# Conformer-and-attention block on one core: the layer norm of the convolution branch finished inside the attention projection, rarer convolution taps, four buffers for the rotated halves, weights recorded with priority

## The chip, the cores and the metric

The kernel runs on one NeuronCore of a Trainium2 chip. The metric is device time in microseconds (us), the median of three runs. The core has a matrix engine (PE, with its weight loads shown as PEld), a vector engine (DVE), a scalar engine (ACT), a third elementwise engine (POOL) and an engine that here only issues transfers (SP). Each engine works through its own list of instructions in order and waits on semaphores for the others.

## The reference

One decoder block on x of 2048 tokens by 1024 channels, all in fp32:

```python
h = rmsnorm(x, norm_g)
glu_in, conv_gate, q, k, v, attn_gate, merge_logits = split(h @ w_in)   # w_in 1024 x 7680
c = silu(layernorm(causal_depthwise_conv31(a * sigmoid(b))))            # a, b = halves of glu_in
y_conv = (c * silu(conv_gate)) @ w_conv_out
att = sliding_window_attention(rope(q), rope(k), v, sinks)              # 16 heads of 64, 4 kv heads, window 128
y_attn = (att * silu(attn_gate)) @ w_attn_out
g_conv, g_attn = split(sigmoid(merge_logits))
out = rmsnorm(x + (g_conv * y_conv + g_attn * y_attn) @ w_out, final_norm_g)
```

## The kernel before

**Sweeps and tiles.** The tokens go in two sweeps of T = 1024, each in two halves of TH = 512. Channels stand on the 128 partitions, so a projection makes one tile of 128 output channels by 512 tokens from KC = 8 tiles of the contraction. fp32 accuracy is kept by splitting each operand into a high and a low part: `project` issues, for each of the eight k, the three matmuls whi x hT_hi, whi x hT_lo, wlo x hT_hi, so 24 matmuls for one half. Names tell the part: `gb`, `ga` the two halves of glu_in, `ka`/`kb`, `v`, `q_a`/`q_b`, then `ag` (attention gate), `cg` (convolution gate), `ma` and `mc` (the two merge gates), `ya` and `yc` (the projections after attention and convolution), `o` (the last one).

**Weights.** `load_w` (lines 244 to 266) fetches a weight tile in two parts: a DMA into `raw` (L250), a cast on ACT into `whi` (L253), and in sweep 0 a subtraction on POOL into `wlo` (L242), which is stored to DRAM (`d_lo`, L263) and fetched from there in sweep 1. The three staging tags have four buffers each. `prefetch` in `project` calls it one projection ahead. A name such as `whi_ma_21` is merge-gate tile 2, second part.

**Order.** PE's order is written by hand: a `Line` (from L80) adds up a modelled time and, between matmuls, calls background operations (`bg`) at a spacing `every` and late chains (attention blocks, layer norm, the gated products `u`) when they fall due. `CONV_EVERY` is that spacing while the 31 convolution taps per channel tile run (L393, DVE), `LN_EVERY` that of the layer norm. The order on ACT, DVE, POOL and SP is made by a scheduler that takes ready work by priority; `tc.high_priority(offset=PRIO)` moves what is recorded inside it ahead by 60 places of priority.

**Stages of a sweep.** Load and normalise x, transposed into hT (in sweep 0 `build_h_first`: sqf L350, ssf L351, xf L354, tpf L361, hT L363 and L364); gb/ga, k, v, q projections with rope (`rope_items`: products `ra` L461, `rb` L467, combined on POOL, then split on ACT and DVE); then attention in 32 blocks (scores `sc` L566, exponentials L584, scaling L589, transposes tpp, `pt` L599, masked copy `pc` L605, `ov` L614, result `ss` L617 to L624) interleaved with ag, ga/gb, cg, ma projections and with the convolution taps; then mc, the layer norm, ya, yc and o.

**Layer norm.** When the last tap is done, `ln_chain` sums over channels with four matmuls (`lnmu`), `ln_center` subtracts the mean from the eight `cv` tiles and adds up the squares (L671 ACT, L672 DVE), `ln_chain2` sums again (`lnvar`), then four reciprocals (L676), eight `ln_apply` (L679 DVE, L680 ACT Silu), then `u_chain` makes uT (L711 and a split), which yc multiplies. `ya_item` writes its gated result `mp[e]` into the home `C[e]`, where `cv` tile e lives till then, so before it writes, it calls `line.finish()` if `u` of tile e is not stored yet. The last weights `wo` take the homes C[k] from `mp`.

Of the kernel before, what the change touches and what calls it, by code (L numbers as in the profile page):

```python
# [12 lines left out]
F32 = mybir.dt.float32  # L13
F32R = mybir.dt.float32r
I32 = mybir.dt.int32
AF = mybir.ActivationFunctionType
ALU = mybir.AluOpType
AX = mybir.AxisListType

P = 128  # L20
S = 2048
D = 1024
KC = D // P
T = 1024
NSWEEP = S // T
NB = T // P
TH = 512
# [15 lines left out]
LN_EVERY = 1.6  # L43
GLU_AFTER = (0, 6, 12, 16, 19, 22, 25, 28)
ROPE_EVERY = 3.2
CONV_EVERY = 2.4
ATT_EVERY = 13.8
LAT = (22.0, 16.0)
PRIO = 60
# [4 lines left out]
def hybrid_block(ctx: ExitStack, tc: tile.TileContext, x, par_d, w_in, w_conv, sinks, w_attn, w_out,  # L54
# [22 lines left out]
    C = [f"c{i}" for i in range(8)]  # L77
# [3 lines left out]
    def slot(tag, shape, dt, name):  # L81
        n = int(np.prod(shape[1:]))
        full = HALO + T + 2 if tag in WIDE else 1024
        t = slots.tile([P, full], dt, tag=tag, name=name)
        v = t[:, 0:n]
        if len(shape) == 3:
            v = v.rearrange("p (a b) -> p a b", b=shape[2])
        elif len(shape) == 4:
            v = v.rearrange("p (a b c) -> p a b c", b=shape[2], c=shape[3])
        return v  # L90
# [6 lines left out]
    def next_of(key, tags):  # L97
        rot.setdefault(key, cycle(range(len(tags))))
        return tags[next(rot[key])]
# [46 lines left out]
    def lng(c):  # L146
        return par[:, c, TAPS + 2:TAPS + 3]

    def lnb(c):
        return par[:, c, TAPS + 3:TAPS + 4]  # L150
# [93 lines left out]
    def load_w(src, name):  # L244

        parts = []
        at = lo_at.setdefault((src.tensor.name, src.offset), len(lo_at))
        for kh in range(2):
            raw = stage.tile([P, 4, P], F32, tag="raw", name=f"raw_{name}{kh}")
            nc.sync.dma_start(out=raw, in_=src[:, 4 * kh:4 * kh + 4, :])  # L250
            hi = stage.tile([P, 4, P], F32R, tag="whi", name=f"whi_{name}{kh}")
            lo = stage.tile([P, 4, P], F32R, tag="wlo", name=f"wlo_{name}{kh}")
            act.copy(hi, raw)  # L253
            if (at, kh) in lo_stored:
                nc.sync.dma_start(out=f(lo), in_=d_lo[at, kh])
            else:
                split_lo(lo, raw, hi, pool)
            parts.append((hi, lo))

        def keep(kh):  # L260
            if (at, kh) not in lo_stored:
                lo_stored.add((at, kh))
                nc.sync.dma_start(out=d_lo[at, kh], in_=f(parts[kh][1]))  # L263

        return lambda k: (parts[k // 4][0][:, k % 4, :], parts[k // 4][1][:, k % 4, :]), keep

    def project(src, rhs, name, evac, halves=(0, 1)):

        got = {}

        def prefetch():
            got["w"] = load_w(src, name)

        def blocks():
            for half in halves:
                ps = mm_ps.tile([P, TH], F32, tag="mm", name=f"mm_{name}{half}")
                for k in range(KC):
                    whi, wlo = got["w"][0](k)
                    r = rhs(k, half)
                    for i, (a, b) in enumerate(((whi, r[:, 0, :]), (whi, r[:, 1, :]), (wlo, r[:, 0, :]))):  # L280
                        pe.matmul(out=ps, lhsT=a, rhs=b, start=(k == 0 and i == 0),  # L281
                                  stop=(k == KC - 1 and i == 2))
                    if k == KC - 1:
                        with tc.high_priority(offset=PRIO):
                            evac(half, ps)
                    if half == halves[-1] and k % 4 == 3:
                        got["w"][1](k // 4)
                    yield 3 * MM_US

        def by_halves():  # L290
            return [project(src, rhs, f"{name}{h}", evac, (h,)) for h in range(2)]

        return prefetch, blocks, by_halves
# [78 lines left out]
    def sweep(s):  # L372
# [82 lines left out]
        def rope_items(name, e, store):  # L455
            first = {}

            def ev_a(half, ps):
                t = first[half] = slot(AT[4 + half], [P, 2, TH], F32, f"ra{s}_{name}_{half}")
                dve.tensor_tensor(out=t[:, 0, :], in0=ps, in1=cs[half][:, 0, :], op=ALU.mult)  # L460
                dve.tensor_tensor(out=t[:, 1, :], in0=ps, in1=cs[half][:, 1, :], op=ALU.mult)  # L461

            def ev_b(half, ps):
                a = first[half]
                b = slot(next_of("rb", [AT[6], AT[13]]), [P, 2, TH], F32, f"rb{s}_{name}_{half}")
                dve.tensor_tensor(out=b[:, 1, :], in0=ps, in1=cs[half][:, 1, :], op=ALU.mult)
                dve.tensor_tensor(out=b[:, 0, :], in0=ps, in1=cs[half][:, 0, :], op=ALU.mult)  # L467
                pool.tensor_tensor(out=a[:, 0, :], in0=a[:, 0, :], in1=b[:, 1, :], op=ALU.subtract)
                pool.tensor_tensor(out=a[:, 1, :], in0=a[:, 1, :], in1=b[:, 0, :], op=ALU.add)
                for i in range(2):  # L470
                    hl = slot(next_of("hl", AT[7:11]), [P, 2, TH], F32R, f"hl{s}_{name}_{half}_{i}")
                    put_split(hl, a[:, i, :], dve)
                    store(i, half, f(hl))

            return [project(w_in[e], h_rhs, f"{name}a{s}", ev_a),
                    project(w_in[e + 1], h_rhs, f"{name}b{s}", ev_b)]
# [184 lines left out]
        def ln_center(c):  # L661
            dve.tensor_tensor(out=cv[c], in0=cv[c], in1=ln["mu"], op=ALU.subtract)
            if c == 0:
                ln["v"] = work.tile([P, T], F32, tag="ln0", name=f"vsum{s}", bufs=1)
            for half in range(2):
                hs = slice(half * TH, (half + 1) * TH)
                if c == 0:
                    act.activation(out=ln["v"][:, hs], in_=cv[c][:, hs], func=AF.Square)
                else:
                    q = t2k(f"sq{s}_{c}_{half}")  # L670
                    act.activation(out=q, in_=cv[c][:, hs], func=AF.Square)  # L671
                    dve.tensor_tensor(out=ln["v"][:, hs], in0=ln["v"][:, hs], in1=q, op=ALU.add)  # L672

        def ln_recip(i):
            r = ln["r"][:, i * (T // 4):(i + 1) * (T // 4)]
# [2 lines left out]
        def ln_apply(c):  # L678
            dve.tensor_tensor(out=cv[c], in0=cv[c], in1=ln["r"], op=ALU.mult)  # L679
            act.activation(out=cv[c], in_=cv[c], func=AF.Silu, scale=lng(c), bias=lnb(c))  # L680

        def ln_chain():
            parts = ln_parts(csum, "csum")
# [10 lines left out]
        def ln_chain2():  # L694
            parts = ln_parts(ln["v"], "vsum")
            yield 0.0, LN_LAT[1]
            st = ln_stats(parts, "lnvar")
            ln["r"] = slot(X[1], [P, T], F32, f"rstd{s}")
            for half in range(2):
                act.activation(out=ln["r"][:, half * TH:(half + 1) * TH], in_=st[half], func=AF.Sqrt, bias=eps)  # L700
            work_ops = [lambda i=i: ln_recip(i) for i in range(4)]
            line.bg.extend(work_ops + [lambda c=c: ln_apply(c) for c in range(KC)])
            line.late.append((line.t, u_chain(), lambda: len(uT) > 0))
            yield 4 * MM_US, 0.0


# [17 lines left out]
        def u_chain():  # L724
            for e in range(KC):
                line.bg.extend([lambda e=e, h=h: u_op(e, h) for h in range(2)])
            return
            yield
# [55 lines left out]
        def ya_item(e, first):  # L784
            def ev(half, ps):
                if half == 0:
                    if ("u", e, 1) not in stored:
                        line.finish()
                    mp[e] = slot(C[e], [P, T], F32, f"mp{s}_{e}")
                g = load_gate("ma", e, half)  # L790
                dve.tensor_tensor(out=mp[e][:, half * TH:(half + 1) * TH], in0=ps, in1=g, op=ALU.mult)

            prefetch, blocks, _ = project(w_attn[e], lambda k, half: aT[half][k],
                                       f"ya{s}_{e}", ev)
            if not first:
                return prefetch, blocks

            def first_blocks():
                start_u()
                if None in aT[0] + aT[1]:  # L800
                    line.finish()
                yield from blocks()

            return prefetch, first_blocks
# [30 lines left out]
        def load_wo(n, k):  # L835
            raw = raw_tile(f"rawo{s}_{n}_{k}")
            nc.sync.dma_start(out=raw, in_=wout[:, k, n * TH:(n + 1) * TH])
            w = slot(C[k], [P, 2, TH], F32R, f"wo{s}_{n}_{k}")
            act.copy(w[:, 0, :], raw)
            split_lo(w[:, 1, :], raw, w[:, 0, :], dve)  # L840
            wo[(n, k)] = w
# [115 lines left out]
```

## Time and profile before

| what | us |
|---|---|
| median of three runs (lowest, highest) | 2090.49 (2089.47, 2090.71) |
| the profiled execution | 2090.34 |
| its span in the trace | 2088.4 |
| PE busy in the span | 2044.0 (98%) |
| DVE, ACT, POOL busy | 1391.3, 1032.4, 483.2 |
| mean granted clock of PE | 0.995 |

The profiled execution stands 0.15 us under the median, and 1.9 us of it lie outside the span. PE is busy for all but 44.4 us of the span, so what a change can save at constant work is in those 44.4 us and in stretches in which the clock of PE is granted at less than full. The line numbers in all rows of before are those of the listing above; in the changed kernel lines behind L272 stand one to three higher.

### The profile page before, as it was taken

To read this page: it belongs to the slowest core of one execution; us is meant where nothing else is said; L and a number is where in the kernel's file an instruction comes from. 1 tells how busy PE (TensorE), PEld (TensorE's weight loads), DVE (VectorE), ACT (ScalarE), POOL (GpSimd) and SP (SyncE) were. 2 spreads that over 40 slices of the span, in tenths; PEclk is the share of its full clock that TensorE was granted. 3 is DMA by queue.
4 is the path that set the end of the run, shared out by engine and by line. 5 is a ranking of instruction groups with operands and counts; after the bars stand their busy time and mean duration, and the time that the engine had idled before them with its cause. 6 is when DMAs were issued, how large, how long until landed. Compare 5 with 4: busy or idle time off the path is not lost.

```text
span 2088.4 us, 27452 instructions
## 1 busy us (share of the span) xinstructions
PE 2044.0 (98%) x9256; PEld 1671.7 (80%) x9256; DVE 1391.3 (67%) x1901; ACT 1032.4 (49%) x2265; POOL 483.2 (23%) x336
## 2 busy tenths in 40 slices
PE   7999999998999999999999999999999999999998
PEld 6787888886777888888888888888888888888887
DVE  4979779998988348123559596698888934341324
ACT  6221377666667646112442214766777774621222
POOL 2445433433334222243001131121111110000200
PEclk9999999999999999999999999999999999999999
DMA  7344555554455775646344456555555578574432
GB/s 250 133 144 157 178 166 157 158 163 146 148 152 182 254 238 184 202 142 221 101 151 132 141 161 204 172 158 175 175 163 164 175 225 259 162 236 146 140 119 81
DMA packets 265820, 355.90 MB, mean 170 GB/s; under 512 B 28112, under 2 KB 126544, under 8 KB 265680
## 3 DMA queue, kind: packets, MB, share of 16 engines
q1 hardware_dynamic: 265680, 354.16, 53.3%
q8 instruction: 73, 1.20, 0.2%
q14 instruction: 67, 0.55, 0.1%
HBM read 234.51 MB, written 119.54 MB: 170 GB/s over the span
## 4 chain that ended last, share of the span: by engine, by line
PE 70%; DVE 4%; issue 2%; ACT 1%; DMA 0%; POOL 0%; SPq 0%; DVEq 0%; POOLq 0%; ACTq 0%
PE o L877 9%; PE mm_mc L281 8%; PE mm_yc L281 8%; PE mm_ya L281 8%; PE mm_ma L281 7%; PE mm_ga L281 5%; PE mm_cg L281 5%; PE mm_ag L281 4%; PE mm_gb L281 4%; DVE cv L393 2%; PE mm_q_a L281 2%; PE mm_q_b L281 2%; PE ov L614 2%; PE sc L566 2%; PE mm_v L281 1%
## 5 line engine op out<-in xcount | busy, mean ns | idle before, releaser
L393 DVE SCALAR_TENSOR_TENSOR cv<-glu,par,cv 128x1024 f32<-128x1024 f32 x480 | 675.9, 1408 | 6.7
L605 POOL TENSOR_SCALAR_AFFINE_SELECT pc<-pt 128x1024 fp32r<-128x1024 f32 x60 | 102.7, 1711 | 452.9 <-DVE pt L242 419.6
L877 PE MATMUL o<-wo,mT 128*128 128x512 f32 x768 | 181.3, 394 | 0.0
L877 PEld LDWEIGHTS o<-wo,mT 128*128 128x128 f32 x768 | 143.1, 188 | 32.1
L281 PE MATMUL mm_cg<-hT,whi_cg 128*128 128x512 f32 x512 | 163.2, 400 | 4.6 <-ACT glu L415 3.0
L281 PE MATMUL mm_ma<-hT,whi_ma 128*128 128x512 f32 x512 | 162.9, 399 | 4.0 <-ACT whi_ma L253 4.0
L281 PE MATMUL mm_ga<-hT,whi_ga 128*128 128x512 f32 x512 | 161.0, 395 | 0.2 <-ACT whi_ga L253 0.2
L281 PE MATMUL mm_ag<-hT,whi_ag 128*128 128x512 f32 x512 | 160.9, 395 | 0.0
L281 PE MATMUL mm_gb<-hT,whi_gb 128*128 128x512 f32 x512 | 160.6, 395 | 0.0
L281 PE MATMUL mm_mc<-hT,whi_mc 128*128 128x512 f32 x512 | 159.6, 393 | 0.0
L281 PE MATMUL mm_yc<-uT,whi_yc 128*128 128x512 f32 x512 | 159.4, 392 | 0.0
L281 PE MATMUL mm_ya<-aT,whi_ya 128*128 128x512 f32 x512 | 158.7, 391 | 0.0
L281 PEld LDWEIGHTS mm_cg<-hT,whi_cg 128*128 128x128 f32 x512 | 95.3, 191 | 25.2 <-ACT glu L415 3.4
L281 PEld LDWEIGHTS mm_ma<-hT,whi_ma 128*128 128x128 f32 x512 | 95.1, 190 | 23.9 <-ACT whi_ma L253 4.4
L281 PEld LDWEIGHTS mm_yc<-uT,whi_yc 128*128 128x128 f32 x512 | 96.2, 188 | 21.9
L281 PEld LDWEIGHTS mm_mc<-hT,whi_mc 128*128 128x128 f32 x512 | 96.0, 188 | 21.8
L281 PEld LDWEIGHTS mm_ya<-aT,whi_ya 128*128 128x128 f32 x512 | 96.1, 188 | 20.9
L281 PEld LDWEIGHTS mm_ga<-hT,whi_ga 128*128 128x128 f32 x512 | 94.5, 188 | 20.8 <-ACT whi_ga L253 1.0
L281 PEld LDWEIGHTS mm_gb<-hT,whi_gb 128*128 128x128 f32 x512 | 94.7, 188 | 20.0
L281 PEld LDWEIGHTS mm_ag<-hT,whi_ag 128*128 128x128 f32 x512 | 94.2, 188 | 19.7 <-ACT whi_ag L253 0.3
L584 ACT ACTIVATE ss<-ss,st 128x128 f32<-128x128 f32 x256 | 99.9, 391 | 19.2 <-DVE st L579 18.6
L815 POOL TENSOR_TENSOR lmc<-lmc,mp 128x512 f32<-128x512 f32 x32 | 41.9, 1309 | 275.5 <-DVE lmc L814 267.1
(363 smaller groups left out, 4356.4 us busy)
## 6 DMA issues: line engine op xcount, KB each, us to landing
qk<-d_q SPq DMA_DIRECT2D x256, 64.0 KB, 2.7
d_a<-ss SPq DMA_DIRECT2D x128, 128.0 KB, 1.9
aT<-d_a SPq DMA_DIRECT2D x32, 512.0 KB, 6.1
qk<-d_k SPq DMA_DIRECT2D x240, 64.0 KB, 2.1
raw_gb<-in_w_in_dram SPq DMA_DIRECT2D x34, 256.0 KB, 4.0
raw_ga<-in_w_in_dram SPq DMA_DIRECT2D x34, 256.0 KB, 3.4
raw_ag<-in_w_in_dram SPq DMA_DIRECT2D x32, 256.0 KB, 3.8
d_ag<-ag SPq DMA_DIRECT2D x32, 256.0 KB, 2.1
```

What stands on the lines that cost most here:

```text
L281: pe.matmul(out=ps, lhsT=a, rhs=b, start=(k == 0 and i == 0), stop=(k == KC - 1 and i == 2))
L393: dve.scalar_tensor_tensor(out=cv[c], in0=glu[c][:, j:j + T], scalar=tap(c, j), in1=cv[c], op0=ALU.mult, op1=ALU.add)
L566: pe.matmul(out=o, lhsT=q[:, h, :], rhs=r, start=(j == 0), stop=(j == 1))
L584: act.activation(out=sb[:, h, :], in_=sb[:, h, :], func=AF.Exp, scale=SCALE, bias=ngm[:, h:h + 1], accum_out=den[:, h:h + 1])
L605: pool.affine_select(out=pc, in_=f(pt), pattern=[[0, 2], [0, GQ], [1, P]], compare_op=ALU.is_ge, fill=0.0, base=0, channel_multiplier=-1)
L614: pe.matmul(out=ov, lhsT=vv, rhs=pp[:, i % 2], start=(i == 0), stop=(i == nm - 1))
L815: pool.tensor_tensor(out=g, in0=g, in1=mp[e][:, half * TH:(half + 1) * TH], op=ALU.add)
L877: pe.matmul(out=ps, lhsT=a[:, c0:c0 + P], rhs=r, start=(k == 0 and i == 0), stop=(k == KC - 1 and i == 2))
```

## The change

Seven edits. The spacing of convolution taps in the line of PE goes from 2.4 to 2.55 us. The prefetch of every projection weight is recorded with priority. `ra` takes its home in turn from four places instead of one per half. Half of the additions of squares (L672, half 1) go from DVE to POOL. `u_chain` waits for all eight `ln_apply`. `mp` gets the homes X[2], X[0], X[1], C[0] to C[4] in place of C[0] to C[7], and the line is finished only for e = 2 when `ln_apply` isn't through, and for e > 2 when `u` of tile e - 3 isn't. `wo` takes C[5], C[6], C[7], C[0] and so on.

```diff
-CONV_EVERY = 2.4
+CONV_EVERY = 2.55
...
         def prefetch():
-            got["w"] = load_w(src, name)
+            with tc.high_priority(offset=PRIO):
+                got["w"] = load_w(src, name)
...
             def ev_a(half, ps):
-                t = first[half] = slot(AT[4 + half], [P, 2, TH], F32, f"ra{s}_{name}_{half}")
+                t = first[half] = slot(next_of("ra", AT[4:6] + C[4:6]), [P, 2, TH], F32, f"ra{s}_{name}_{half}")
...
-                    dve.tensor_tensor(out=ln["v"][:, hs], in0=ln["v"][:, hs], in1=q, op=ALU.add)
+                    (dve, pool)[half].tensor_tensor(out=ln["v"][:, hs], in0=ln["v"][:, hs], in1=q, op=ALU.add)
...
             act.activation(out=cv[c], in_=cv[c], func=AF.Silu, scale=lng(c), bias=lnb(c))
+            if c == KC - 1:
+                stored.add("applied")
...
-            line.late.append((line.t, u_chain(), lambda: len(uT) > 0))
+            line.late.append((line.t, u_chain(), lambda: len(uT) > 0 and "applied" in stored))
...
-                    if ("u", e, 1) not in stored:
+                    if e > 2 and ("u", e - 3, 1) not in stored or e == 2 and "applied" not in stored:
                         line.finish()
-                    mp[e] = slot(C[e], [P, T], F32, f"mp{s}_{e}")
+                    mp[e] = slot(([X[2], X[0], X[1]] + C)[e], [P, T], F32, f"mp{s}_{e}")
...
-            w = slot(C[k], [P, 2, TH], F32R, f"wo{s}_{n}_{k}")
+            w = slot(C[(k + 5) % KC], [P, 2, TH], F32R, f"wo{s}_{n}_{k}")
```

What this makes of the order is shown at four places. The first is SP's list at the very start: `xf` are the eight row blocks of x, `raw_gb_000` and `_001` the first weight tile. Before:

```order
L107 DMA xf_0_80<-in_x_dram 128x1024
L107 DMA xf_1_82<-in_x_dram 128x1024
L107 DMA xf_2_84<-in_x_dram 128x1024
L107 DMA xf_3_86<-in_x_dram 128x1024
L133 DMA sink_bc<-in_attn_sinks_dram 128x16
L136 DMA par<-in_par_dram 128x280
L453 DMA cs_0_133<-in_rope_dram 128x2x512
L453 DMA cs_1_135<-in_rope_dram 128x2x512
L250 DMA raw_gb_000_137<-in_w_in_dram 128x512
L250 DMA raw_gb_001_143<-in_w_in_dram 128x512
```

and now:

```order
L250 DMA raw_gb_000_137<-in_w_in_dram 128x512
L250 DMA raw_gb_001_143<-in_w_in_dram 128x512
L107 DMA xf_0_80<-in_x_dram 128x1024
L107 DMA xf_1_82<-in_x_dram 128x1024
L107 DMA xf_2_84<-in_x_dram 128x1024
L107 DMA xf_3_86<-in_x_dram 128x1024
L133 DMA sink_bc<-in_attn_sinks_dram 128x16
```

The two weight parts have moved ahead of x. The second place is ACT's list some 20 us later, where the last tiles of the first half of hT are evacuated (`hT_0_6`, `hT_0_7`), the squares of the second half's rows are summed (`sqf`) and the next weights are cast. Before:

```order
L363 ACTIVATE hT_0_6_130<-tpf_6_220,par 128x512
L351 ACTIVATE ssf_234<-ssf_234,eps_t 128x1
L350 ACTIVATE sqf_1_240,ssf_234<-xf_1_151 128x1024
L363 ACTIVATE hT_0_7_131<-tpf_7_227,par 128x512
L351 ACTIVATE ssf_234<-ssf_234,eps_t 128x1
L350 ACTIVATE sqf_2_245,ssf_234<-xf_2_153 128x1024
L350 ACTIVATE sqf_3_250,ssf_234<-xf_3_155 128x1024
L351 ACTIVATE ssf_234<-ssf_234,eps_t 128x1 x2
L253 CAST whi_ga_000_257<-raw_ga_000_255 128x512
```

and now:

```order
L364 ACTIVATE hT_0_6_130<-tpf_6_220,par 128x512
L352 ACTIVATE ssf_234<-ssf_234,eps_t 128x1
L351 ACTIVATE sqf_2_245,ssf_234<-xf_2_153 128x1024
L351 ACTIVATE sqf_3_250,ssf_234<-xf_3_155 128x1024
L253 CAST whi_ga_000_257<-raw_ga_000_255 128x512
L253 CAST whi_ga_001_263<-raw_ga_001_261 128x512
L352 ACTIVATE ssf_234<-ssf_234,eps_t 128x1 x2
L253 CAST whi_ka_299<-raw_ka_297 128x512
L364 ACTIVATE hT_0_7_131<-tpf_7_227,par 128x512
L253 CAST whi_ka_305<-raw_ka_303 128x512
```

`hT_0_7` now stands behind two sums of squares, two roots and three weight casts. The third place is ACT's list in the attention of sweep 0, at the second part of merge-gate tile 2. Before:

```order
L584 ACTIVATE ss_3_1_5355,st_3_1_5358<-ss_3_1_5355,st_3_1_5358 128x128 x3
L599 CAST pt_3_0_5437<-tpp_3_0_5431 128x512
L434 ACT_TABLE_LOAD
L434 ACTIVATE ma_1_0_5443<-mm_ma_10_5407 128x512
L589 ACTIVATE ss_3_1_5355<-ss_3_1_5355,st_3_1_5358 128x128 x4
L617 COPY ss_2_7_5081<-ov_2_7_5457 64x256
L253 CAST whi_ma_21_5403<-raw_ma_21_5401 128x512
```

and now:

```order
L585 ACTIVATE ss_3_1_5346,st_3_1_5349<-ss_3_1_5346,st_3_1_5349 128x128
L253 CAST whi_ma_21_5394<-raw_ma_21_5392 128x512
L585 ACTIVATE ss_3_1_5346,st_3_1_5349<-ss_3_1_5346,st_3_1_5349 128x128 x2
L435 ACT_TABLE_LOAD
L435 ACTIVATE ma_1_0_5434<-mm_ma_10_5398 128x512
L600 CAST pt_3_0_5428<-tpp_3_0_5422 128x512
L590 ACTIVATE ss_3_1_5346<-ss_3_1_5346,st_3_1_5349 128x128 x4
L618 COPY ss_2_7_5070<-ov_2_7_5448 64x256
```

The cast has moved ahead of the scaling L589 and stands among the exponentials; in the same way the casts of ag_61, ga_41, cg_71, gb_71, ga_71 and ma_01 have moved ahead by a few places. The fourth place is PE's list in sweep 0, at the two groups of layer-norm matmuls. Before, the second group stood in merge-gate tile `mc` 6:

```order
L281 MATMUL mm_mc_60_6894<-hT_0_1_125,wlo_mc_60_6813 128x512
L658 MATMUL lnvar_0_6901<-vsumh_0_6708,ones 128x512
L658 MATMUL lnvar_0_6901<-vsuml_0_6709,ones 128x512
L658 MATMUL lnvar_1_6904<-vsumh_1_6712,ones 128x512
L658 MATMUL lnvar_1_6904<-vsuml_1_6713,ones 128x512
L281 MATMUL mm_mc_60_6894<-hT_0_2_126,whi_mc_60_6812 128x512 x2
```

and now it stands in the second half of the first tile of `ya`:

```order
L282 MATMUL mm_ya_01_7079<-aT_1_5_6726,wlo_ya_01_6961 128x512
L659 MATMUL lnvar_0_7099<-vsumh_0_6921,ones 128x512
L659 MATMUL lnvar_0_7099<-vsuml_0_6922,ones 128x512
L659 MATMUL lnvar_1_7102<-vsumh_1_6925,ones 128x512
L659 MATMUL lnvar_1_7102<-vsuml_1_6926,ones 128x512
L282 MATMUL mm_ya_01_7079<-aT_1_6_6754,whi_ya_01_6960 128x512 x2
```

The first group (`lnmu`) has moved in the same way from `mc` 2 to behind the first half of `mc` 5, and in sweep 1 both groups move by about as much. PE's list is otherwise the same. DVE's list keeps its order through rope, and in attention single taps move by one or two places. In the layer norm the half-1 additions are gone from DVE, and the first four `mp` products of `ya` now stand among the reciprocals, the `ln_apply` products and `u`.

## Prediction

> **What bounds the kernel now.** I read the page first, then PE's waits, then stretches, then single moments. PE's row of the page:
>
> ```profile
> PE 2044.0 (98%) x9256; PEld 1671.7 (80%) x9256; DVE 1391.3 (67%) x1901; ACT 1032.4 (49%) x2265; POOL 483.2 (23%) x336
> ```
>
> PE is busy for 2044.0 of 2088.4 us, so the change, which takes no matmul away, can give at most the idle 44.4 us and what a lowered clock costs. The longest of PE's waits behind the head, up to 700 us (engine, line, waited for; us in total, times, longest):
>
> ```profile
> PE mm_ma L281 <- ACT whi_ma L253: 4.0, 1, 4.0
> PE mm_q_b L281 <- DVE rb_q__1_1524 L467: 3.4, 1, 3.4
> PE mm_cg L281 <- ACT glu L415: 3.0, 1, 3.0
> PE tpv L499 <- ACT vs L519: 2.1, 1, 2.1
> PE mm_cg L281 <- POOL wlo_cg L242: 2.0, 1, 2.0
> PE mm_ga L281 <- POOL wlo_ga L242: 1.8, 2, 1.2
> ...
> PE mm_gb L281 <- POOL wlo_gb L242: 1.5, 1, 1.5
> ...
> PE mm_ag L281 <- POOL wlo_ag L242: 1.3, 1, 1.3
> PE mm_q_b L281 <- DVE ra_q__0_1408 L461: 1.3, 1, 1.3
> ...
> PE mm_ma L281 <- POOL wlo_ma L242: 0.6, 1, 0.6
> ```
>
> Six of these rows name a weight part (whi or wlo): 4.0 + 2.0 + 1.8 + 1.5 + 1.3 + 0.6 = 11.2 us, all in the attention of sweep 0. The rest are evacuations (glu, vs) and rope. The stretches (start and length, then busy us of PE, PEld, DVE, ACT, POOL, PE's granted clock, DMA share, GB/s):
>
> ```profile
> 140.00:211.00 71.00, 65.78 (x277) 52.67 (x276) 69.87 (x58) 10.38 (x18) 32.39 (x20) 0.98 0.46 145
> 235.00:640.00 405.00, 386.72 (x1793) 314.95 (x1792) 363.74 (x467) 274.97 (x636) 147.48 (x96) 0.98 0.52 158
> 550.00:560.00 10.00, 8.04 (x35) 6.38 (x34) 9.90 (x14) 4.25 (x10) 5.65 (x3) 0.83 0.44 134
> 620.00:630.00 10.00, 6.03 (x29) 4.71 (x27) 9.82 (x13) 9.46 (x22) 0.09 (x1) 0.95 0.60 180
> 630.00:640.00 10.00, 9.87 (x33) 7.39 (x34) 9.90 (x14) 6.17 (x17) 4.64 (x3) 0.71 0.30 91
> 720.00:1000.00 280.00, 280.00 (x1226) 228.67 (x1225) 114.93 (x148) 97.41 (x160) 81.54 (x60) 1.00 0.59 196
> 1073.00:2080.00 1007.00, 1007.00 (x4571) 827.31 (x4570) 643.12 (x893) 491.46 (x1066) 126.64 (x83) 1.00 0.54 169
> ```
>
> The last row says that sweep 1 has no gap on PE: nothing is to be had there. Rope (140 to 211) and attention (235 to 640) are where PE idles, and there DVE is busy for 69.87 of 71 and 363.74 of 405 us.
>
> **The change part by part.**
>
> **The head: a loss.** Rows of the first 30 us:
>
> ```profile
> 4.28 1.06 ACT L350 ACTIVATE sqf<-xf 128x1024 f32<-128x1024 f32 x1 [1.98 <-DMA xf<-in_x_dram]
> 5.69 1.06 ACT L350 ACTIVATE sqf<-xf 128x1024 f32<-128x1024 f32 x1
> 15.55 1.13 ACT L253 CAST whi_gb<-raw_gb 128x512 fp32r<-128x512 f32 x2
> 18.52 0.70 PE L281 MATMUL mm_gb<-hT,whi_gb 128*128 128x512 f32 x2
> 20.57 0.69 ACT L363 ACTIVATE hT<-tpf,par 128x512 fp32r<-128x512 f32 x1
> 21.30 0.75 DVE L364 SCALAR_TENSOR_TENSOR hT<-tpf,par,hT 128x512 fp32r<-128x512 f32 x1 [0.19 <-ACT hT L363]
> 23.78 0.62 ACT L253 CAST whi_ga<-raw_ga 128x512 fp32r<-128x512 f32 x1
> 24.45 0.73 PE L281 MATMUL mm_ga<-hT,whi_ga 128*128 128x512 f32 x2 [0.21 <-ACT whi_ga L253]
> 25.87 0.50 PE L281 MATMUL mm_ga<-hT,wlo_ga 128*128 128x512 f32 x1 [0.70 <-POOL wlo_ga L242]
> ```
>
> and of DVE's waits behind the head, up to 700 us, the one for PE:
>
> ```profile
> DVE glu L419 <- PE mm_ga L281: 23.9, 5, 9.3
> ```
>
> The first weight tile (two parts of 128x512, as many bytes as one row block of x) now loads ahead of x. Two row blocks start on ACT 5.69 - 4.28 = 1.4 us apart, so x comes about 1.4 us later; the two whi_gb casts (1.1 us) no longer stand in x's way at 15.55, so mm_gb starts some 0.3 us later, at 18.8. The larger part is `hT_0_7`. Its evacuation stood at 20.57; now it follows both last sqf, the roots, two whi_ga casts and a whi_ka cast. In before ACT had the sums and roots done at 23.78; without the 0.69 of hT_0_7 ahead, and 0.3 later, that is 23.4. Three casts of 0.62 bring hT_0_7's start to 25.3 and its end to 26.0, its low part (DVE, 0.75) to 26.7. mm_gb needs it at its eighth k: one k takes (24.24 - 18.52) / 8 = 0.7 (mm_ga starts at 24.45 after 0.21 of waiting), so at 18.8 + 4.9 = 23.7. PE waits 2.3, and another 0.5 for the low part. Against that the waits for whi_ga and wlo_ga (0.21 + 0.70) go, since their casts now come first. 0.3 + 2.3 + 0.5 - 0.9 = 2.2; with hT of the second half behind the same evacuations I take +2.5. Bounds: +0.3 if only x's shift stays, and 2.5 + 1.7 = 4.2 if the wait also draws a stretch at half clock (550 to 560 lost (1 - 0.83) x 10 = 1.7). Nothing later swallows it: five times DVE stands idle for a ga projection (23.9 us in all), the last of them just ahead of attention, so up to there what PE loses the others lose too.
>
> [...] In the trace the stretch 550 to 560, with the wait of 2.0 us for wlo_cg in it, shows a lowered clock (0.83). [...]
>
> **Weights with priority in attention: the gain.** Around the longest wait:
>
> ```profile
> 627.64 1.28 ACT L589 ACTIVATE ss<-ss,st 128x128 f32<-128x128 f32 x4 [0.43 <-DVE st L587]
> ...
> 629.22 1.14 ACT L253 CAST whi_ma<-raw_ma 128x512 fp32r<-128x512 f32 x2
> ...
> 629.89 1.22 PE L281 MATMUL mm_ma<-hT,whi_ma 128*128 128x512 f32 x2 [3.98 <-ACT whi_ma L253]
> ```
>
> PE waited for whi_ma_21, which stood on ACT behind L589, which waited for DVE. Now the cast stands among the exponentials, some 5 us earlier, and the wait goes. So do the other five of the six rows, whose casts moved too. At their largest they are worth 11.2 us and the clock of the three 10-us stretches above (1.7 + 0.5 + 2.9 = 5.1): 16.3 us. But PE cannot come so far ahead of the rest:
>
> ```profile
> 593.25 0.60 ACT L415 ACTIVATE glu<-mm_gb 128x512 f32<-128x512 f32 x1
> 595.46 0.63 PE L281 MATMUL mm_ma<-hT,whi_ma 128*128 128x512 f32 x2
> 659.40 2.10 POOL L605 TENSOR_SCALAR_AFFINE_SELECT pc<-pt 128x1024 fp32r<-128x1024 f32 x1
> 667.30 0.62 PE L614 MATMUL ov<-pt,vt 128*128 128x512 f32 x2
> ```
>
> mm_ma at 595.46 takes the PSUM buffer that glu leaves at 593.85: 1.6 us of slack. ov at 667.30 reads pc, done at 661.50: 5.8. What paces these is a chain over ACT, DVE and POOL that does not wait for PE:
>
> ```profile
> DVE pt L242 <- ACT pt L599: 24.5, 8, 3.8
> ```
>
> DVE's largest sum of waits is this one, for ACT, and none of them is for PE between 235 and 640; the exponentials and taps go on at their own pace, so a gap closed early is met again at the next evacuation, and what counts is what is left at the chain's end, near 667: 5.8 us. Most of it can come from the one gap at 630 (4.0 and the clock of 630 to 640, 2.9), whose neighbours have the room. I take -5.8, with the ends 0 (the chain comes as much later as the casts now stand ahead of it) and -16.3.
>
> **Taps at 2.55.** The list of DVE shows taps moved by a place or two: the number of taps and their order against PE's matmuls stay, so 0; within the bounds of the term above, since any shift of a tap is a shift of the same chain.
>
> **Four ra buffers.** The rope waits in the rows above are 3.4 and 1.3. DVE is busy for 69.87 of the 71 us, and its order there is unchanged: it never stood idle for a free ra, so more buffers give 0. Ends: 0 and -4.7.
>
> **Layer norm, mp, wo.** PE's matmuls are the same in number; lnvar moves by some 31 us (780.0 to 811). Rows:
>
> ```profile
> 780.01 0.39 PE L658 MATMUL lnvar<-vsumh,ones 128*128 128x512 f32 x1
> ...
> 838.13 0.68 DVE L242 TENSOR_TENSOR uT<-lcg,uT 128x512 fp32r<-128x512 f32 x1
> ...
> 889.63 0.63 PE L281 MATMUL mm_yc<-uT,whi_yc 128*128 128x512 f32 x2
> ```
>
> From lnvar to the last low part of u took 58.1 us; 811 + 58 = 869 leaves 20 us before yc. The mp products now stand in DVE's list among this, with DVE busy for only 114.93 of 280 us; half of the additions of squares on POOL, busy for 81.54 of 280, take from DVE what it has to spare. The new condition on u_chain delays only u, which has the same 20 us. lnmu and lnvar hold two of three PSUM buffers for about 1 us inside mc and ya, as before inside mc. wo's first three homes are free earlier (no mp in them). All 0; ends: 0, and +5.5 (one half of a tile, 8 x 0.7) if one evacuation came too late.
>
> **Sum.** 2090.34 + 2.5 - 5.8 = 2087.0 for an execution like the profiled one; the median lies 0.15 higher: 2087.2. A measurement of this kernel tells 0.2% (4.2 us) from no change, so this is "the same", near the edge of faster (2086.3).
>
> **The rivals.**
> *The chain does not bind* and all six weight waits and the clock go: 2090.5 + 2.5 - 16.3 = 2076.7. For it: all six casts did move, and ACT has idle time (274.97 busy of 405 us) in which evacuations could come earlier. Against it: the slack of 1.6 at 595 and 5.8 at 667. Partial forms lie between 2086 and 2077.
> *A cast that waits takes the place of the gap* (slower). ACT works in order, and a cast placed ahead of exponentials holds them up while its raw part is on the way. The trace has one such case, harmless where it stood since nothing urgent was behind it:
>
> ```profile
> ACT whi_ag L253 <- DMA raw_ag<-in_w_in_dram: 10.5, 1, 10.5
> ```
>
> Put before the exponentials of one attention block it delays the chain by its length; with 10.5 the total is 2087.2 + 10.5 = 2097.7. It decides from 7.5 us on, where the sum passes +4.2. Against it: the scheduler places a cast when it holds its part for landed.
> *The gain is 1.6 us only*, the slack at 595, and the head's loss stays: 2090.5 + 2.5 - 1.6 = 2091.4.
> *The change doesn't do what it says* holds for ra and the taps already in my sum.
>
> **How the numbers follow.** My forecast has 0.42, spread from 2084.5 to 2089.5 by the head's bounds; a third of it falls below 2086.3. The unbound chain and its partial forms 0.20, the small gain 0.18, the waiting cast (or a like delay of the chain) 0.20. Faster: 0.14 + 0.20 = 0.34; same: 0.28 + 0.18 = 0.46; slower: 0.20. The range 2079 to 2096 leaves out the far half of the unbound chain and the far half of the slower rival, together 0.2.
>
> **What would show it.** Head right: PE waits for hT at about 24 us, 2 to 3 us in all, and the second half's transposes come about 2.5 us later. Gain right: no row of PE waiting for whi_ma or wlo, no clock of 0.71 near 630, PE's remaining waits for glu, cg or pc. Rope right: the two waits for rb and ra are there as before. Layer norm right: PE busy for all of 720 to 1000. Wrong: a DVE that idles in rope, an ACT that waits for raw between exponentials, or a gap of PE in ya.

## The result: slower, and the profile after

The changed kernel takes 2108.24 us (median of five; 2107.93 to 2109.57) against 2090.71 for the kernel before beside it: a ratio of 1.0084, with a 95% interval of 1.0072 to 1.0096. That is 17.5 us more, where 3 us less was forecast and 2096 was the upper end.

The page of the changed kernel, its span and PE's row:

```profile
span 2106.1 us, 27349 instructions
...
PE 2051.1 (97%) x9256; PEld 1673.1 (79%) x9256; DVE 1395.0 (66%) x1887; ACT 1017.0 (48%) x2253; POOL 506.2 (24%) x350
```

PE has the same 9256 matmuls and 55 us of idle time in place of 44.4. Its waits in the first 31 us, the longest ones from 31 to 720 us, and all behind 720 us (engine, line, waited for; us in total, times, longest):

```profile
PE tpf L362 <- DVE ident_r L117: 10.3, 1, 10.3
...
PE mm_gb L282 <- ACT hT L364: 1.9, 1, 1.9
PE mm_gb L282 <- DVE hT L365: 1.7, 1, 1.7
...
PE mm_ma L282 <- ACT glu L416: 3.5, 1, 3.5
PE mm_q_b L282 <- DVE rb_q__1_1524 L468: 3.4, 1, 3.4
PE sc L567 <- DVE ss L575: 3.0, 4, 1.1
PE mm_cg L282 <- ACT glu L416: 2.9, 1, 2.9
...
PE mm_q_b L282 <- DVE ra_q__0_1408 L462: 1.3, 1, 1.3
...
PE mm_ga L282 <- POOL wlo_ga L242: 1.0, 1, 1.0
PE mm_ma L282 <- POOL wlo_ma L242: 0.9, 1, 0.9
...
PE lnvar L659 <- DVE mp L794: 5.3, 1, 5.3
PE mm_ya L282 <- ACT mc L435: 0.9, 1, 0.9
```

The weight waits fell from 11.2 us to 1.9 as intended. New are the two for hT in the head, one of 3.5 for an evacuation (glu, at mm_ma), longer ones for masked scores (ss, 3.0 in place of 1.0), and the one of lnvar in ya. All of PE's waits between 31 and 720 us add up to 25.3 us, in before to 25.6: what the weights no longer cost there, evacuations and scores do. The stretches of the changed kernel (columns as before):

```profile
24.00:34.00 10.00, 6.34 (x19) 4.66 (x18) 4.08 (x6) 6.10 (x12) 5.88 (x4) 0.70 0.46 147
820.00:830.00 10.00, 4.69 (x14) 3.43 (x13) 0.69 (x1) 2.58 (x4) 0.94 (x1) 0.66 0.63 207
720.00:1000.00 280.00, 273.83 (x1185) 222.76 (x1184) 113.27 (x133) 88.89 (x146) 100.53 (x71) 0.99 0.60 199
1095.00:2095.00 1000.00, 1000.00 (x4535) 821.44 (x4534) 637.78 (x869) 479.32 (x1048) 136.28 (x88) 1.00 0.54 169
```

Sweep 1 (last row) is without a gap, as before. So all of the loss is in sweep 0, and the start of the same matmul in the two traces says where:

| matmul | before, us | after, us | later by | grown since the row above |
|---|---|---|---|---|
| mm_ga_000, third k | 27.35 | 33.66 | 6.3 | 6.3, the head |
| mm_ma_51, first (behind the last waits of attention) | 675.32 | 683.94 | 8.6 | 2.3, rope and attention |
| mm_ya_01, eighth k | 812.16 | 828.96 | 16.8 | 8.2, mc and ya |
| the end (span) | 2088.4 | 2106.1 | 17.7 | 0.9 |

Three losses, then; each of them was forecast at another size: +2.5, -5.8 and 0. The border between the first two is not sharp. PE's clock is still low at the third k of mm_ga_000; at the fourth, where it is full again, the two traces are 6.8 us apart (28.40 and 35.21), so 0.5 of the 2.3 belongs to the head.

**The head.** Rows of ACT, PE and DVE of the changed kernel:

```profile
7.60 1.06 ACT L351 ACTIVATE sqf<-xf 128x1024 f32<-128x1024 f32 x1 [2.49 <-DMA xf<-in_x_dram]
20.01 0.70 PE L282 MATMUL mm_gb<-hT,whi_gb 128*128 128x512 f32 x2
26.24 0.69 ACT L364 ACTIVATE hT<-tpf,par 128x512 fp32r<-128x512 f32 x1
26.93 1.57 DVE L355 TENSOR_SCALAR xf<-xf,ssf 128x1024 f32<-128x1024 f32 x1
28.43 0.74 DVE L365 SCALAR_TENSOR_TENSOR hT<-tpf,par,hT 128x512 fp32r<-128x512 f32 x1
```

The first rows of x came 3.3 us later (7.60 against 4.28), mm_gb 1.5 us later (20.01 against 18.52). hT_0_7 was about as late on ACT as worked out (26.24 to 26.93; its end was forecast at 26.0), but its low part stood on DVE behind a scaling of x that took 1.57 us, so PE waited 1.7 more, not 0.5. (That scaling, the last of four, took 1.58 in before too, but there the low part of hT_0_7 stood ahead of it.) And behind the two waits stands a stretch at a lowered clock: 0.70 over the ten microseconds of the row above, and, read in steps of one, 0.50 from 28 to 34. Over the ten that is (1 - 0.70) x 10 = 3.0 us at most, since PE stood idle for a part of it. By the starts it is 2.6: the 6.8 at the fourth k, less 1.5 for mm_gb and the two waits of 1.9 and 1.7, plus the 0.9 of the two weight waits that went.

**The layer norm inside ya.** Rows of ACT, DVE and PE:

```profile
815.42 0.60 ACT L435 ACTIVATE mc<-mm_mc 128x512 f32<-128x512 f32 x1 [6.94 <-DMA d_mc<-mc]
...
818.14 0.60 ACT L435 ACTIVATE mc<-mm_mc 128x512 f32<-128x512 f32 x1 [1.10 <-DMA d_mc<-mc]
...
825.49 0.69 DVE L794 TENSOR_TENSOR mp<-mm_ya,lma 128x512 f32<-128x512 f32 x1 [16.89 <-DMA lma<-d_ma]
...
826.23 0.80 PE L659 MATMUL lnvar<-vsumh,ones 128*128 128x512 f32 x1 [5.31 <-DVE mp L794]
```

This reads backwards. The second lnvar group needs the PSUM buffer that mp_0 empties; mp_0 waits for the load of `lma`; that load needs one of the five `t2k` buffers; four hold the high and low parts of vsum, which only lnvar sets free; the fifth is passed from mc_7_0 to mc_7_1 to lma, each behind the other's transfer. Why mc 7 was still on its way at 815 is seen a little earlier, in the additions of squares (groups of the layer norm, first before, then two rows after; xcount, busy us, mean ns):

```profile
L672 DVE TENSOR_TENSOR vsum<-vsum,sq 128x512 f32<-128x512 f32 x14 | 10.9, 831 | 0.0
```

```profile
L673 POOL TENSOR_TENSOR vsum<-vsum,sq 128x512 f32<-128x512 f32 x7 | 13.8, 1970 | 2.4 <-ACT sq L672 2.2
L673 DVE TENSOR_TENSOR vsum<-vsum,sq 128x512 f32<-128x512 f32 x7 | 11.2, 1605 | 0.2
```

Half of the additions on POOL did not halve DVE's work: seven took 11.2 us where fourteen had taken 10.9, since each was twice as long beside POOL's: six of the seven took 1.6 to 1.8 us, where one without POOL beside it takes 0.68. From the first subtraction of the mean to the last part of vsum it is 25.9 us in place of 22.5. One thing more stands in this trace and no run tried it: the first of the two stores of mc, issued at 809.05, stood behind a load of 512 KB for the last stage (`gb`, issued at 808.63).

### The profile page after: what moved, and what is told of

It is laid out like the page before. It is cut to its first block, busy times and chain, and to the rows that moved or that the text cites. A ratio compares the mean times of both kernels' runs of the same rounds, so it can differ in the third digit from the quotient of the medians.

```text
span 2106.1 us, 27349 instructions
## 1 busy us (share of the span) xinstructions
PE 2051.1 (97%) x9256; PEld 1673.1 (79%) x9256; DVE 1395.0 (66%) x1887; ACT 1017.0 (48%) x2253; POOL 506.2 (24%) x350
## 4 chain that ended last, share of the span: by engine, by line
PE 67%; DVE 6%; ACT 1%; issue 1%; POOL 1%; DMA 1%; SPq 0%; DVEq 0%; POOLq 0%; ACTq 0%
PE o L880 8%; PE mm_yc L282 8%; PE mm_ya L282 8%; PE mm_mc L282 7%; PE mm_ma L282 6%; PE mm_cg L282 6%; PE mm_ag L282 4%; PE mm_ga L282 4%; PE mm_gb L282 4%; DVE cv L394 3%; PE mm_q_a L282 2%; PE mm_q_b L282 2%; PE ov L615 2%; PE sc L567 2%; PE mm_v L282 1%
## 5 line engine op out<-in xcount | busy, mean ns | idle before, releaser
L282 PE MATMUL mm_ga<-hT,wlo_ga 128*128 128x512 f32 x256 | 101.3, 396 | 1.0 <-POOL wlo_ga L242 1.0
```

## The experiments

All ratios are to the kernel before on the same chip, whose medians there were 2090.6 to 2091.5.

**e1: a sixth t2k buffer.** In the changed kernel:

```diff
-        return work.tile([P, TH], dt, tag="t2k", name=name, bufs=5)
+        return work.tile([P, TH], dt, tag="t2k", name=name, bufs=6)
```

> The changed kernel with six t2k buffers in place of five. Theory: vsumh/vsuml hold four of the five till lnvar, which now stands in ya, so mc_7_0, mc_7_1 and lma_0_0 pass one after the other through the fifth, each behind the other's transfer, and mp_0 and with it lnvar's PSUM buffer come 5.3 us late. A sixth buffer breaks that line: the waits of 5.3 and 0.9 and the lowered clock at 820 to 830 go, about 8 us, 2100. Rival: it is PSUM, two of the three buffers taken by lnmu/lnvar: no change, 2108.

Measured 2103.23 (ratio 1.0059, 1.0046 to 1.0072): 5.0 less, not 8. lnvar waits 2.0 us for mp_0 instead of 5.3. The buffer count is a part of it and not the whole.

**e2: no priority for the first six weight tiles.** In the changed kernel's prefetch:

```diff
+            if len(lo_at) < 6:
+                got["w"] = load_w(src, name)
+                return
             with tc.high_priority(offset=PRIO):
```

> The changed kernel with priority only from the seventh weight tile on. Theory: the 6.6 us by which PE is late at 35 us come from the first weights alone (raw_gb ahead of x, casts ahead of hT_0_7) and reach the end: mm_gb starts at 18.5 again, 2101.6. Rival: the chain in attention has a pace of its own and takes part of it back: 2104 to 2108.

Measured 2102.36 (1.0054, 1.0042 to 1.0067), 5.9 less: the head's loss comes from these tiles and is carried to the end almost whole. mm_ga_000 stands where it stood in before.

**e3: taps at 2.4 again.**

```diff
-CONV_EVERY = 2.55
+CONV_EVERY = 2.4
```

> The changed kernel with the taps at 2.4 again. PE's list is then that of before, lnmu and lnvar in mc. Theory 1 (spacing moves only the layer norm): the 8 us of ya go, attention is as late as in the changed kernel, 2100. Theory 2 (the wider spacing also makes the attention chain 6.5 us later): PE reaches mc up to 6 us earlier than the changed kernel as well, 2094 to 2096.

Measured 2110.70 (1.0095, 1.0082 to 1.0109): neither. PE's list is that of before, and it is no faster than the changed kernel (four runs, 2108.06 to 2113.49). Its waits:

```profile
PE lnvar L659 <- ACT mc L435: 5.2, 3, 2.4
...
PE mm_mc L282 <- ACT mc L435: 2.9, 2, 2.4
```

So the loss is not bound to ya; it goes with the layer norm wherever that stands, which brought the additions on POOL under suspicion. (In attention e3 is as late as the changed kernel, 683.95 at mm_ma_51: the spacing of taps costs nothing there.)

**e4: no priority at all.** The changed kernel with the prefetch of before.

> The changed kernel without priority for the weights. Head as before (-6.6). Theory 1 (the casts ahead of pt and L590 make the attention chain later): attention as in before, gap of 4.0 at whi_ma_21 included; only the 8 us in ya stay: 2098.5. Theory 2 (the spacing of taps does it): the chain stays late and the weight gaps come back: 2102 or more.

Measured 2098.25 (1.0037, 1.0025 to 1.0049), the time of theory 1. Priority costs 10.0 us in this kernel: 5.9 in the head (e2) and 4.1 behind it. That it is the casts which do it, as theory 1 also says, this run does not show, since the priority moves POOL's work along with them.

**e5: priority for one tile.** The kernel before, with `high_priority` only where the name is `ma0_2` (merge-gate tile 2 of sweep 0).

> The kernel before with priority for one weight tile alone, merge-gate tile 2 of sweep 0, whose cast PE waited 4.0 us for at 630. Theory: the head, the taps and the layer norm stay as before, the gap at 630 and its lowered clock go, and PE keeps what the slack at 667 leaves: -4 to -6, 2085 to 2087. Rival: the cast among the exponentials holds up the chain, and PE waits a little later for ov or tpp instead: 2089 to 2091.

Measured 2089.03 (0.9990, 0.9981 to 0.9998), 2.5 less by the medians. The gap at 630 is gone and PE is up to 7.2 us ahead there; what it then meets is

```profile
PE mm_ma L285 <- ACT ma L438: 1.3, 1, 1.3
```

at mm_ma_51, after which it is 4.5 us ahead in the trace. The slack of 5.8 at 667 was nearly the right bound in size, though what PE met was an evacuation of ma and not the pc of that sum. Another 1.8 are given back at 768, where the layer norm's first matmuls wait for an evacuation of mc; 2.3 reach the end of the span.

**e6 and e7: a one-input operation in the place of POOL's subtraction.** In the kernel before, and in e2:

```diff
-                split_lo(lo, raw, hi, pool)
+                pool.tensor_copy(out=lo, in_=f(hi))
```

> The kernel before, but POOL fills wlo by a copy of whi, an operation with one input in place of two; the low part of the weights is therefore not computed. Theory (taps run slower beside a POOL operation with two inputs): the 186 taps between 235 and 700 us take less than their 261.6 us, near 255, and PE's weight waits change with POOL's durations only. Rival (DVE does not care what POOL does): 261 us again.

> The changed kernel with priority from the seventh weight tile on (e2_nohead), and the same copy on POOL for wlo; the low part of the weights is not computed. Theory: what made the chain 6 us later was POOL's two-input subtractions moved beside taps (267.6 against 261.6 us for the same 186 taps): with a one-input copy the taps take as long as in e6_before_onein and the chain at 640 is at most 1 us behind it. Rival (it is the casts ahead of pt and L590 on ACT): the chain is still some 6 us behind.

e6 took 2053.43 (0.9821, 0.9808 to 0.9834) and e7 2057.99 (0.9841, 0.9828 to 0.9855). DVE's taps between 235 and 700 us (busy us and count in the first column behind the length), in this order: before, e2, e6, e7, one fence each:

```profile
235.00:700.00 465.00, 261.58 (x186) 0.00 (x0) 14.55 (x6) 0.99 0.54 166
```

```profile
235.00:700.00 465.00, 267.56 (x186) 0.00 (x0) 14.52 (x6) 1.00 0.53 162
```

```profile
235.00:700.00 465.00, 238.86 (x179) 0.00 (x0) 14.55 (x6) 1.00 0.57 179
```

```profile
235.00:700.00 465.00, 240.30 (x179) 0.00 (x0) 14.57 (x6) 1.00 0.57 178
```

With priority the same 186 taps take 6.0 us longer; with a one-input copy on POOL they are shorter (1.33 us each instead of 1.41) and priority adds 1.4 only. But the copy is also half as long, 0.61 us where the subtraction takes 1.30, so these runs alone do not tell which of the two counts. Single rows do. One such tap, in e2, with POOL's subtraction beside it (two taps in one row: 3.66, where two take 2 x 1.28):

```profile
279.37 1.29 POOL L242 TENSOR_TENSOR wlo_gb<-raw_gb,whi_gb 128x512 fp32r<-128x512 f32 x1 [9.96 <-ACT whi_gb L253]
...
279.41 3.66 DVE L397 SCALAR_TENSOR_TENSOR cv<-glu,par,cv 128x1024 f32<-128x1024 f32 x2
```

The same in before, and in e6 with the copy, a tap and POOL's operation starting together:

```profile
529.78 1.29 POOL L242 TENSOR_TENSOR wlo_cg<-raw_cg,whi_cg 128x512 fp32r<-128x512 f32 x1
...
529.79 2.36 DVE L393 SCALAR_TENSOR_TENSOR cv<-glu,par,cv 128x1024 f32<-128x1024 f32 x1
```

```profile
301.94 0.61 POOL L257 CAST wlo_ag<-whi_ag 128x512 fp32r<-128x512 f32 x1 [0.63 <-ACT whi_ag L253]
...
301.92 1.71 DVE L393 SCALAR_TENSOR_TENSOR cv<-glu,par,cv 128x1024 f32<-128x1024 f32 x1
```

A tap is stretched beside the one-input copy too, and the two stretched taps differ (2.36 - 1.71 = 0.65) by about as much as the two POOL operations (1.29 - 0.61 = 0.68). The masked copy pc, which has one input, behaves alike. Here it is in before, first alone (708), then beside two taps (321), then in an odd case (281):

```profile
708.10 1.10 POOL L605 TENSOR_SCALAR_AFFINE_SELECT pc<-pt 128x1024 fp32r<-128x1024 f32 x1
...
321.52 2.07 POOL L605 TENSOR_SCALAR_AFFINE_SELECT pc<-pt 128x1024 fp32r<-128x1024 f32 x1 [3.08 <-DVE pt L242]
...
321.37 3.31 DVE L393 SCALAR_TENSOR_TENSOR cv<-glu,par,cv 128x1024 f32<-128x1024 f32 x2
...
281.71 2.47 POOL L605 TENSOR_SCALAR_AFFINE_SELECT pc<-pt 128x1024 fp32r<-128x1024 f32 x1 [10.14 <-DVE pt L242]
...
281.95 1.27 DVE L393 SCALAR_TENSOR_TENSOR cv<-glu,par,cv 128x1024 f32<-128x1024 f32 x1
```

At 321 pc took 2.07 where it takes 1.10 alone, since the first tap was running, and the second tap took 2.0 (3.31 less 1.28) behind pc. At 281 pc started while a short operation on DVE was still running, the tap got its turn ahead of pc, and pc alone was stretched. So the two took turns: of the 40 taps of before that started during a subtraction for a weight, 35 ended 1.08 to 1.09 us behind it (the other five started in its last 0.1 us), 34 of the 35 that started during pc ended 1.07 to 1.08 behind it (the other is the case at 281), and the tap of e6 above ended 1.08 behind the copy (303.63 against 302.55). What counted here is how long POOL's operation was and not how many inputs it had; the theory of e6 and e7 had the collision right and its condition wrong.

The expectation for e7 held for PE, which stands up to 2 us ahead of e6 between 600 and 740, but not for the chain: one tap in the middle of the last channel tile, at 627 in before, comes 6.6 us later in e2 than in before and still 3.4 us later in e7 than in e6. In e2 the longer taps up to there make up 6.4 of the 6.6, in e7 1.4 of the 3.4. So POOL beside the taps accounts for nearly all of the chain's delay in e2 by size. What makes the rest in e7 stays open; the casts ahead of pt and L590 on ACT were not tried by themselves. By the medians e7 takes 4.6 us more than e6; in the traces PE falls behind e6 in ya, where e7 keeps the additions of squares on POOL.

**e8: e3 with all additions on DVE.**

```diff
-                    (dve, pool)[half].tensor_tensor(out=ln["v"][:, hs], in0=ln["v"][:, hs], in1=q, op=ALU.add)
+                    dve.tensor_tensor(out=ln["v"][:, hs], in0=ln["v"][:, hs], in1=q, op=ALU.add)
```

> The changed kernel with taps at 2.4 (e3_conv24) and all additions of squares on DVE again. In e3_conv24 PE lost 8 us in mc of sweep 0 and 4 in sweep 1, behind ACT's evacuations of mc. Theory 1 (ACT's copies of vsum wait for POOL's additions and mc's evacuation stands behind them): the loss goes, 2099 to 2100. Theory 2 (t2k buffers, held by vsumh and vsuml till lnvar, as in ya): most of it stays, 2106 or more.

Measured 2100.08 (1.0043, 1.0030 to 1.0057): 10.6 less than e3, and PE no longer waits in mc. Theory 1.

**e9: the changed kernel with all additions on DVE.** The same edit.

> The changed kernel with all additions of squares on DVE. Theory 1 (POOL's additions stretch the layer norm's middle, ACT's sums of squares wait for them, and the evacuations of mc 6 and 7 stand behind these on ACT, so t2k buffers and with them mp_0 come late): the 8 us in ya go, 2099 to 2101. Theory 2 (the one t2k buffer left by vsumh and vsuml is enough of a cause): lnvar waits for mp_0 all the same, 2106 or more.

Measured 2101.02 (1.0050, 1.0036 to 1.0064), 7.2 less: theory 1 again. What lnvar still waits:

```profile
PE lnvar L659 <- DVE mp L794: 1.3, 1, 1.3
```

**e10: e9 without priority for the first six tiles.**

> e9 with priority only from the seventh weight tile on. What is then left of the loss is that of the attention chain: before + 2, that is 2093. If the parts do not add up, 2096 or more.

Measured 2095.66 (1.0022, 1.0013 to 1.0031), 2.7 above the 2093 expected: the parts undone add to 12.6 of the 5.9 + 7.2 = 13.1, and 5.0 us stay. By the trace 3.4 of them are there at mm_ma_51 (rope and attention) and about 2 come in ya, 1.2 of these as lnvar's wait.

**e11: only the additions on POOL.** The kernel before with that one edit.

> The kernel before with half of the additions of squares on POOL, that edit alone. Theory 1: lnmu and lnvar stand in mc, and the loss is that of e3_conv24 against e8_conv24_dve, +8 in sweep 0 and +3 in sweep 1, 2101 to 2103. Rival (the loss needs the priority of the weights as well): under 2095.

Measured 2098.93 (1.0037, 1.0025 to 1.0050), 8.3 more with no priority anywhere. PE's waits behind 700 us:

```profile
PE lnvar L658 <- ACT mc L434: 4.6, 2, 3.3
PE mm_mc L281 <- ACT mc L434: 1.4, 2, 1.2
```

The size is 2 us under the expected 2101 to 2103 and well over the rival's 2095; the split is not as expected: by the start of the same matmuls 3.4 us are lost in sweep 0 and 5.4 in sweep 1.

**e12: the rest of the change, and priority for one tile.** The changed kernel with all additions on DVE and priority for `ma0_2` alone; spacing 2.55, four ra buffers and the homes of mp and wo stay.

> The changed kernel with all additions on DVE and priority for merge-gate tile 2 of sweep 0 alone. It keeps the spacing of 2.55, the four ra buffers and the new homes of mp and wo. Theory (these cost and give nothing): as e5_ma2, 2088 to 2090. Rival (the layer norm inside ya still costs some us): 2092 or more.

Measured 2087.67 (0.9985, 0.9976 to 0.9994): faster than both kernels, by 0.15% than the one before. Neither lnmu nor lnvar waits here, so moving the layer norm behind costs nothing by itself, and the 1.8 us that e5 gave back at 768 are kept: 3.5 us reach the end of the span (2084.9 against 2088.4; 3.0 by the medians). Against e10, which has priority on every tile from the seventh on in place of this one, it is 8.0 less. Whether the time is better than e5's the intervals don't tell.

## Why the prediction was wrong, step by step

- **Layer norm, mp, wo: "All 0".** This is the step that failed most: 8.2 us. Two sentences of it were wrong. That POOL's additions "take from DVE what it has to spare" looked at busy shares; additions on both engines at once took turns, so that one on DVE took twice as long (a mean of 831 ns became 1605), ACT's sums of squares and evacuations stand behind them, and undoing this edit alone gave 7.2 (e9). And the count of buffers looked at PSUM only. Five t2k buffers, four of them held by vsum, were short as well: a sixth gave 5.0 (e1), and that the two gains overlap (5.0 + 7.2 is more than 8.2) says that either relief shortens the same line. The end named, +5.5 for one evacuation too late, was the right event; the lowered clock behind it (0.66 in 820 to 830) made it larger. In the trace of before ACT already waited six times, 11.7 us in all, for a store of mc to free its buffer; that row would have shown that the buffers were short.
- **The head: +2.5, measured +6.3** (6.8 one k later; 5.9 in time, e2). The mechanism was right, hT_0_7 on ACT to within 1 us. Three sizes were off: x by 3.3 in place of 1.4 at its first row block, of which 1.5 reached mm_gb (0.3 forecast); the low part's DVE queue (1.7 for 0.5); and the clock, 2.6, taken as a bound of 1.7 only. That bound was read from one gap: in before the clock stood at 0.50 from 554 to 557, behind 2.0 us without work for PE, and here it stood at 0.50 from 28 to 34, behind two gaps of 1.9 and 1.7.
- **Weights with priority in attention: -5.8, measured +2.3.** The weight waits went (11.2 to 1.9) and the gap at 630 closed; the slack bound held in e5 (4.5 of 5.8). What failed is that the exponentials and taps "go on at their own pace": priority moved POOL's subtractions beside other taps too, and the chain came 6.6 us later (e2), 6.4 of it in longer taps. Whether the casts ahead of the exponentials add to it stays open. The end 0 for this term had that delay in it as a parenthesis, with no price. The rival "a cast that waits" had its sign and not its mechanism: in attention ACT waited 4.9 us for a raw part, where it had waited 10.5 in before.
- **Contention of POOL and DVE** was in the trace of before and was not read: taps of 1.28 us and a mean of 1.41. Alone a tap took 1.28 us, beside a subtraction 2.36 (before, at 529.79). On POOL's side the count of inputs made no difference: a one-input copy stretched a tap to 1.71 (e6).
- **Taps, ra, mp and wo homes: 0.** Right. The rope waits are the 3.4 and 1.3 of before, and e12 keeps all of these edits and is not slower.
- **Sweep 1: nothing.** Right for the changed kernel; with the layer norm in mc (e11) it would not have been.

## What to carry to other kernels

An operation that moves from one elementwise engine to another is not priced by the idle share of the one that takes it. Here taps and additions on DVE took turns with the operations on POOL (a tap of 1.28 us took 2.36, an addition of 0.68 took up to 1.80), so work moved to POOL still held up DVE where the two met; look in the trace for two lengths of the same operation, and for what runs beside the long one. Before a priority is put on a whole class of work, ask which engine's work it pulls along and what that will stand beside; here one tile with priority gave 2.5 us (e5) and all of them cost 10 in the changed kernel (e4). And count every pool that a stretched lifetime passes through, the small ring of staging buffers too: here its last free buffer turned independent transfers into a line, and a sixth buffer gave 5.0 us (e1).

## What the runs showed of the hardware that was not expected

In these traces a tap, an addition of squares or a subtraction of the mean on DVE and an operation on POOL (subtraction, addition, masked copy, copy) took turns: the second of the two ended about its own time behind the end of the first (in before a tap of 1.28 us 1.08 behind, a masked copy of 1.10 0.96 behind). A tap of 1.28 us took 2.36 beside a subtraction of 1.29 and 1.71 beside a copy of 0.61; POOL's masked copy took 2.07 or 2.47 beside a tap in place of 1.10. Additions of squares of 0.68 us took 1.6 to 1.8, subtractions of the mean of 1.21 up to 2.33. One input or two on POOL made no difference, its length did.

Replacing the subtractions of sweep 0 by a copy half as long moved the kernel from 2091.54 to 2053.43 us: more than all of PE's idle time behind the head, with PE's clock at 0.999 in place of 0.995. The copy also needs less of POOL's own time (0.61 us in place of 1.30), and PE, which waits 7.9 us for low parts of weights in before, has no such wait in e6; how much of the 38 us is that and how much is the taps was not taken apart.

Behind two idle gaps of PE of 1.9 and 1.7 us close together stood some 6 us at half the clock (0.50 from 28 to 34 in the changed kernel).
